# Reading the scalar 1.0 of VectorE's two-operand instructions from SBUF in a decoder layer

## The chip, the cores and the metric

The kernel runs on one core of one Trainium2 chip. The metric is the device time of one execution in microseconds (us), lower is better; the median of several runs counts. Five engines work side by side: TensorE (PE in the rows, with PEld for its weight loads), VectorE (DVE), ScalarE (ACT), GpSimd (POOL) and SyncE (SP), which issues all the DMAs of this kernel. Each takes its own instructions in order.

## What is computed

One decoder layer over 4096 positions of 1024 channels in float32. Two heads share one input projection: a causal depthwise convolution of width 31, and a spatial gate over chunks of 128 positions.

```
h = layer_norm(x)
a_val, a_gate, a_z, b_u, b_v, b_z = split(h @ w_in)          # six times 512 columns
y_a = silu(layer_norm(conv31(a_val * sigmoid(a_gate)))) * silu(a_z)
y_b = gelu(b_u) * (masked_ws @ layer_norm(gelu(b_v)) + b_s) * silu(b_z)
h = layer_norm(2**0.25 * h + concat(y_a, y_b) @ w_out)
out = h + sigmoid(h @ w_ple_gate + b) * (p @ w_ple)
```

## The kernel before

Five matrix products of 4096x1024 by 1024x1024 ("units" 0 to 4) run one after another, 16 pairs of 128-row tiles each. Every product is cut into quarters and done with seven block products in place of eight (Strassen's scheme in Winograd's form); `ORDER` names the seven. To hold float32 accuracy, each operand is split into a high and a low part, `ahi`/`alo` on the left and `whi`/`wlo` on the right, and three matmuls (lines 316 to 318) stand for one.

Three things are made on the side. The weights' seven combinations of the next unit are computed by GpSimd in `combos` (tile `bq`), stored in DRAM (`twD`) and fetched at the end of a unit by `load_operands` (tile `wst`), where ScalarE makes `whi` and VectorE `wlo` (`split_weight`). The left operands come by DMA (`qa`, `qb` from `qD`) or from transposed rows. The convolution (`conv`, lines 388 to 399) runs on VectorE with PSUM accumulators `acc`; its taps are per-partition scalars read from the SBUF tiles `cs_sb` and `cw_sb`. Tiles of the pool tag "big" (7 buffers, `wst`, `bq`, `qa`, `xr` and others) are shared by all stages.

A helper `ss` stands for `out = a op b` on two SBUF operands; it is written as VectorE's scalar_tensor_tensor, (a * 1.0) op b. It is called for `wlo` (two halves of 128x1024 for each weight operand), for the first combinations of weights (`wst`), for the rows of the first two pairs (`xr`), for the norm of v in unit 1 (`v`), for the low parts of the last product's small operands (`pl`, `wpl`, `wsx`), and for the last add of the output rows (`zr`). All of these appear in the trace as line 93, the helper's own.

The order of the instructions on each engine is not written out by hand. A scheduler of the language, with costs of its own for each instruction, orders the whole program when it is built, and chooses the buffers; a small change can reorder much of it.

Of the kernel before, what the change touches and what calls it, by code (L numbers as in the profile page):

```python
# [8 lines left out]
F32 = mybir.dt.float32  # L9
# [3 lines left out]
ADD, SUB, MUL = ALU.add, ALU.subtract, ALU.mult  # L13
# [3 lines left out]
P = 128  # L17
# [47 lines left out]
def hybrid_layer_kernel(  # L65
# [17 lines left out]
    nc = tc.nc  # L83
# [4 lines left out]
    stt = nc.vector.scalar_tensor_tensor  # L88
    ID = AF.Identity

    def ss(out, a, b, op):

        return stt(out, a, 1.0, b, op0=MUL, op1=op)  # L93

    const = ctx.enter_context(tc.tile_pool(name="const", bufs=1))
    dram = ctx.enter_context(tc.tile_pool(name="dram", bufs=1, space=DRAM))
# [28 lines left out]
    make_identity(nc, ident)  # L125
    nhalf = const.tile([P, 2], F32, name="nhalf")
    nc.gpsimd.memset(nhalf, -0.5)
    cw_sb = const.tile([P, CT, W31], F32, name="cw_sb")
    cs_sb = const.tile([P, CT, NE], F32, name="cs_sb")
    cb_sb = const.tile([P, CT], F32, name="cb_sb")  # L130
# [41 lines left out]
    def split_weight(stg):  # L172
        hi, lo = wtile("whi"), wtile("wlo")
        for c in range(2):
            cs = slice(2 * c, 2 * c + 2)
            act(hi[:, cs], stg[:, cs], ID)
            ss(flat(lo[:, cs]), flat(stg[:, cs]), flat(hi[:, cs].bitcast(F32)), op=SUB)
        return hi, lo
# [34 lines left out]
    def first_operands(W, stg):  # L213
        b11, b12, b22, b21 = (stg[ij] for ij in ((0, 0), (0, 1), (1, 1), (1, 0)))

        def sub(dst, a, b):
            for c in range(2):
                cs = slice(2 * c, 2 * c + 2)
                ss(flat(dst[:, cs]), flat(a[:, cs]), flat(b[:, cs]), op=SUB)

        W[1] = split_weight(b11)
        sub(b11, b12, b11)
        W[5] = split_weight(b11)
        W[3] = split_weight(b22)
        sub(b12, b22, b12)
        sub(b22, b22, b11)
        W[6] = split_weight(b22)
        W[7] = split_weight(b12)
        W[2] = split_weight(b21)
        sub(b21, b21, b22)  # L230
        W[4] = split_weight(b21)
# [239 lines left out]
    def first_rows():  # L471

        r = X[0]
        for j in (1, 0):
            mv = mvtile(1)
            moments([r[:, j, 0:C], r[:, j, C:]], mv[:, 0, :])
            nb = scale_bias(mv)
            act(r[:, j], r[:, j], ID, scale=mv[:, 0, 1:2], bias=nb[:, 0:1])
            for half in (0, 1):
                v = r[:, j, half * C : (half + 1) * C]  # L480
                ss(v, v, eb[:, 0, half * C : (half + 1) * C], op=MUL)
                ss(v, v, eb[:, 1, half * C : (half + 1) * C], op=ADD)
            dma(hT[0][j], r[:, j])
# [82 lines left out]
    for h in range(2):  # L566
        half = wsf[64 * h : 64 * (h + 1)].rearrange("p n (i m) -> p n i m", i=2)
        nc.gpsimd.affine_select(
            out=half, in_=half, pattern=[[0, NH], [1, 2], [2, 64]], compare_op=ALU.is_ge,
# [323 lines left out]
```

## Time and profile before

| | |
|---|---|
| median of 3 runs | 1895.17 us (1889.53 to 1897.29) |
| the profiled execution | 1896.8 us, of which its span is 1895.0 us |
| PE busy | 1802.0 us, 95% |
| DVE busy | 1405.1 us, 74%, 2176 instructions |
| POOL busy | 1270.2 us, 67% |
| ACT busy | 893.4 us, 47% |
| DMA | 362.07 MB, 55.4% of 16 engines' span |

The span is the time from the first to the last instruction in the profile; the execution's own time is 1.8 us longer. Busy times are averages over stages with different limits, so the chain of waits (what released the last instruction, followed back) says more of what a slower instruction costs.

### The profile page before, as it was taken

How to read it: one execution, taken by the hardware profiler on the slowest of the kernel's cores; microseconds unless marked ns; L12 is line 12 of the kernel's file. 1: busy time of each engine (PE TensorE's matmuls, PEld its weight loads, DVE VectorE, ACT ScalarE, POOL GpSimd, SP SyncE). 2: the span in 40 equal slices, each digit the busy share in tenths (PEclk: the TensorE clock that was granted, in tenths of full speed). 3: DMA queues.
4: the chain of work that ended last, by engine and by line, in shares of the span. 5: the costliest groups of instructions: out<-in, count | busy, mean ns of one | idle time of the engine just before them, and what ended most of it. 6: DMA issues, size and time to landing. Idle time of an engine off the chain costs nothing.

```text
span 1895.0 us, 24385 instructions
## 1 busy us (share of the span) xinstructions
PE 1802.0 (95%) x8322; PEld 1471.8 (78%) x8322; DVE 1405.1 (74%) x2176; ACT 893.4 (47%) x1438; POOL 1270.2 (67%) x1015
## 2 busy tenths in 40 slices
PE   5799999999999999999999798999999899999999
PEld 3687788877788887788888677787887688888887
DVE  8636887797787777989889976886568756655654
ACT  4655565565455555634445544455546322332222
POOL 2878987458786676588669567776677755655541
PEclk9899999999999999999999998999999999999999
DMA  6579776586734444899666856755446322222211
GB/s 240 193 233 352 254 231 214 182 297 210 239 112 148 138 160 150 304 353 328 211 200 222 308 192 228 250 186 191 168 167 236 119 101 78 89 90 95 100 55 52
DMA packets 184940, 363.62 MB, mean 192 GB/s; under 512 B 49648, under 2 KB 74224, under 8 KB 177136
## 3 DMA queue, kind: packets, MB, share of 16 engines
q1 hardware_dynamic: 184816, 362.07, 55.4%
q8 instruction: 66, 1.08, 0.2%
q14 instruction: 58, 0.48, 0.1%
HBM read 211.02 MB, written 150.99 MB: 191 GB/s over the span
## 4 chain that ended last, share of the span: by engine, by line
PE 75%; DVE 10%; DMA 7%; ACT 3%; issue 3%; POOL 2%; SPq 0%; DVEq 0%; POOLq 0%; ACTq 0%
PE pb L316 9%; PE pb L317 9%; PE pb L318 9%; PE pe L318 6%; PE pe L316 6%; PE pe L317 6%; PE pp L809 5%; PE tp L261 3%; PE pd L316 3%; PE pd L317 3%; PE pd L318 3%; PE pa L316 3%; PE pa L317 3%; PE pa L318 3%; DVE wlo L93 2%
## 5 line engine op out<-in xcount | busy, mean ns | idle before, releaser
L236 POOL TENSOR_TENSOR alo<-s,ahi 128x512 fp32r<-128x512 f32 x192 | 266.7, 1402 | 275.5 <-ACT ahi L235 271.6
L316 PE MATMUL pb<-whi,ahi 128*128 128x512 f32 x960 | 386.8, 403 | 13.2 <-ACT pa L334 5.4
L317 PE MATMUL pb<-wlo,ahi 128*128 128x512 f32 x960 | 379.3, 395 | 1.9 <-DVE wlo L93 1.9
L318 PE MATMUL pb<-whi,alo 128*128 128x512 f32 x960 | 379.0, 395 | 0.1
L316 PE MATMUL pe<-whi,ahi 128*128 128x512 f32 x640 | 257.0, 402 | 16.8 <-ACT ahi L235 7.5
L317 PE MATMUL pe<-wlo,ahi 128*128 128x512 f32 x640 | 253.3, 396 | 4.2 <-DVE wlo L93 4.0
L318 PE MATMUL pe<-whi,alo 128*128 128x512 f32 x640 | 255.5, 399 | 1.6 <-POOL alo L236 1.5
L316 PEld LDWEIGHTS pb<-whi,ahi 128*128 128x128 f32 x960 | 183.1, 191 | 57.0 <-ACT pa L334 9.0
L318 PEld LDWEIGHTS pb<-whi,alo 128*128 128x128 f32 x960 | 182.7, 190 | 40.0 <-POOL alo L236 0.5
L317 PEld LDWEIGHTS pb<-wlo,ahi 128*128 128x128 f32 x960 | 183.2, 191 | 38.8 <-DVE wlo L93 2.9
L236 POOL TENSOR_TENSOR alo<-qa,ahi 128x512 fp32r<-128x512 f32 x128 | 171.5, 1355 | 44.9 <-ACT ahi L235 44.8
L390 DVE SCALAR_TENSOR_TENSOR acc<-ca,cs_sb,acc 128x512 f32<-128x512 f32 x240 | 180.0, 750 | 4.1
L235 ACT ACTIVATE ahi<-s 128x512 fp32r<-128x512 f32 x192 | 119.9, 629 | 131.6 <-DVE s L288 49.7
L399 DVE SCALAR_TENSOR_TENSOR acc<-ca,cw_sb,acc 128x512 f32<-128x512 f32 x240 | 179.1, 746 | 0.8 <-POOL ca L383 0.6
L396 DVE SCALAR_TENSOR_TENSOR acc<-zy,cw_sb,acc 128x512 f32<-128x512 f32 x224 | 167.0, 746 | 2.6 <-POOL zy L382 1.5
L316 PEld LDWEIGHTS pe<-whi,ahi 128*128 128x128 f32 x640 | 121.8, 190 | 42.2 <-ACT ahi L235 8.7
L236 POOL TENSOR_TENSOR alo<-qb,ahi 128x512 fp32r<-128x512 f32 x96 | 126.9, 1328 | 39.6 <-ACT ahi L235 38.8
L317 PEld LDWEIGHTS pe<-wlo,ahi 128*128 128x128 f32 x640 | 121.7, 190 | 30.3 <-DVE wlo L93 6.5
L236 DVE TENSOR_TENSOR alo<-tp,ahi 128x512 fp32r<-128x512 f32 x144 | 97.9, 684 | 62.1 <-ACT ahi L235 60.0
L318 PEld LDWEIGHTS pe<-whi,alo 128*128 128x128 f32 x640 | 121.7, 190 | 26.8 <-POOL alo L236 2.5
L316 PE MATMUL pd<-whi,ahi 128*128 128x512 f32 x320 | 129.9, 406 | 5.5 <-ACT pd L334 3.8
L163 POOL TENSOR_TENSOR mv<-mv,nhalf 128x2 f32<-128x2 f32 (+1 forms) x81 | 55.4, 690 | 108.6 <-DVE mv L162 108.0
(147 smaller groups left out, 3994.7 us busy)
## 6 DMA issues: line engine op xcount, KB each, us to landing
qa<-qD SPq DMA_DIRECT2D x32, 1024.0 KB, 6.2
twD<-bq SPq DMA_DIRECT2D x112, 256.0 KB, 5.8
wst<-twD SPq DMA_DIRECT2D x28, 1024.0 KB, 7.2
qb<-qD SPq DMA_DIRECT2D x32, 768.0 KB, 6.5
xr<-in_x SPq DMA_DIRECT2D x32, 512.0 KB, 5.6
hT<-xr SPq DMA_DIRECT2D x32, 512.0 KB, 3.8
qD<-s SPq DMA_DIRECT2D x64, 256.0 KB, 2.9
bq<-in_wq SPq DMA_DIRECT2D x64, 256.0 KB, 5.0
```

The lines of the kernel that those rows point to most:

```text
L93: return stt(out, a, 1.0, b, op0=MUL, op1=op)
L163: ptt(mv[:, :, 1], mv[:, :, 1], nhalf[:, 0:n], op=ALU.pow)
L235: act(hi, src, ID)
L236: eng.tensor_tensor(lo, src, hi.bitcast(F32), op=SUB)
L261: nc.tensor.transpose(out=tp[:, kk * P : (kk + 1) * P], in_=rows[:, j, k * P : (k + 1) * P], identity=ident,)
L316: nc.tensor.matmul(ps, lhsT=ah[:, k, :], rhs=wh[:, k, :], start=start and k == 0, stop=False, **kw)
L317: nc.tensor.matmul(ps, lhsT=ah[:, k, :], rhs=wl[:, k, :], start=False, stop=False, **kw)
L318: nc.tensor.matmul(ps, lhsT=al[:, k, :], rhs=wh[:, k, :], start=False, stop=k == 3, **kw)
L390: stt(even, src, w, even, op0=MUL, op1=ADD)
L396: stt(dst, src, cw_sb[:, ct, 2 * k + 1 : 2 * k + 2], odd if k else even, op0=MUL, op1=ADD)
L399: stt(src if k == NE - 1 else even, src, cw_sb[:, ct, 2 * k : 2 * k + 1], even, op0=MUL, op1=ADD,)
L809: nc.tensor.matmul(pp, lhsT=l[:, k, ts], rhs=r[:, k, cs], start=k == 0 and l is ph and r is wp_hi, stop=k == 1 and l is pl,)
```

## The change

The helper's immediate 1.0 becomes a pointer to a 128x1 tile `one`, which GpSimd fills once at the start.

```diff
     def ss(out, a, b, op):
 
-        return stt(out, a, 1.0, b, op0=MUL, op1=op)
+        return stt(out, a, one, b, op0=MUL, op1=op)
...
     nhalf = const.tile([P, 2], F32, name="nhalf")
     nc.gpsimd.memset(nhalf, -0.5)
+    one = const.tile([P, 1], F32, name="one")
+    nc.gpsimd.memset(one, 1.0)
     cw_sb = const.tile([P, CT, W31], F32, name="cw_sb")
```

Lines behind the new tile have numbers two higher in the changed kernel.

In the built program the tile `one` takes 32 bytes of each partition, so nearly every SBUF tile lies 32 bytes higher: the first tile of the tag "big" begins at byte 2016 of the partition before and at byte 2048 now, and the others of that tag follow at steps of 8192. The built program also has another order in places: 406 lines of difference in VectorE's 2178 rows, 1290 in TensorE's 8324, 142 in SyncE's 841. Two places follow.

On VectorE, at the end of the start phase, before: the last rows of the second pair's layer norm (`xr`, four instructions of 128x1024) and the last low parts of unit 0's weights (`wlo`).

```order
L162 TENSOR_SCALAR mv<-mv 128x2
L152 BN_AGGR mv<-st 128x2 x2
L93 SCALAR_TENSOR_TENSOR wst<-wst 128x1024 x2
L162 TENSOR_SCALAR mv<-mv 128x2
L93 SCALAR_TENSOR_TENSOR xr<-xr,eb 128x1024 x3
L93 SCALAR_TENSOR_TENSOR wlo<-wst,whi 128x1024
L93 SCALAR_TENSOR_TENSOR xr<-xr,eb 128x1024
L93 SCALAR_TENSOR_TENSOR wlo<-wst,whi 128x1024
```

The same place of the changed kernel, with `one` among the operands:

```order
L164 TENSOR_SCALAR mv<-mv 128x2
L154 BN_AGGR mv<-st 128x2
L93 SCALAR_TENSOR_TENSOR wst<-wst,one 128x1024
L154 BN_AGGR mv<-st 128x2
L93 SCALAR_TENSOR_TENSOR wst<-wst,one 128x1024
L164 TENSOR_SCALAR mv<-mv 128x2
L93 SCALAR_TENSOR_TENSOR xr<-xr,one,eb 128x1024
L93 SCALAR_TENSOR_TENSOR wlo<-wst,one,whi 128x1024
L93 SCALAR_TENSOR_TENSOR xr<-xr,one,eb 128x1024 x2
L93 SCALAR_TENSOR_TENSOR wlo<-wst,one,whi 128x1024
L93 SCALAR_TENSOR_TENSOR xr<-xr,one,eb 128x1024
```

The last of the four `xr` instructions stood behind one `wlo` and now stands behind two.

On SyncE, early in unit 1, before: `uD` stores the gate's tile `g`, `qa` and `qb` fetch the left operands of a coming pair, `bq` and `twD` belong to the weights' combinations.

```order
L187 DMA bq<-in_wq 128x512 x4
L590 DMA uD_133<-g_4170 128x4x512
L190 DMA twD_174<-bq 128x512
L242 DMA qa<-qD_113 128x2048
L190 DMA twD_174<-bq 128x512 x2
L243 DMA qb<-qD_113 128x1536
L192 DMA twD_174<-bq 128x512
L195 DMA twD_174<-bq 128x512
```

The same place now:

```order
L189 DMA bq<-in_wq 128x512 x4
L192 DMA twD_176<-bq 128x512
L244 DMA qa<-qD_115 128x2048
L592 DMA uD_135<-g_4172 128x4x512
L192 DMA twD_176<-bq 128x512 x2
L194 DMA twD_176<-bq 128x512
L197 DMA twD_176<-bq 128x512
L245 DMA qb<-qD_115 128x1536
```

The store `uD` has moved behind the fetch of `qa`, and the fetch of `qb` behind two more stores of `twD`.

## Rows read from the trace of the kernel before

**Rows 1.** The page: busy times, and the chain that ended last by engine.

```profile
PE 1802.0 (95%) x8322; PEld 1471.8 (78%) x8322; DVE 1405.1 (74%) x2176; ACT 893.4 (47%) x1438; POOL 1270.2 (67%) x1015
PE 75%; DVE 10%; DMA 7%; ACT 3%; issue 3%; POOL 2%; SPq 0%; DVEq 0%; POOLq 0%; ACTq 0%
```

**Rows 2.** Windows: start phase and last unit, all engines (columns in the first line).

```profile
core 0: us, PE busy (x) PEld busy (x) DVE busy (x) ACT busy (x) POOL busy (x), PEclk, DMA share, GB/s
0.00:60.00 60.00, 27.00 (x83) 18.75 (x84) 51.58 (x65) 28.89 (x34) 22.07 (x26) 0.89 0.55 200
...
1480.00:1895.00 415.00, 404.51 (x1865) 330.98 (x1863) 248.15 (x336) 115.74 (x194) 215.33 (x114) 0.99 0.24 83
```

**Rows 3.** One line, L93: durations min/median/max in ns, by tile.

```profile
L93 DVE SCALAR_TENSOR_TENSOR wlo<-wst,whi x70: 1164/1218/3379, 13.7 to 1475.4; 128x1024 fp32r<-128x1024 f32 x70
L93 DVE SCALAR_TENSOR_TENSOR v<-v,sgb x64: 655/693/1784, 438.9 to 769.2; 128x512 f32<-128x512 f32 x64
L93 DVE SCALAR_TENSOR_TENSOR zr<-zr,c x32: 682/1372/2893, 1488.7 to 1885.9; 128x512 f32<-128x512 f32 x32
```

**Rows 4.** Windows of L93 alone, whole span: busy us (instructions), PEclk, DMA share, GB/s.

```profile
0.00:1895.00 1895.00, 273.37 (x237) 0.98 0.56 192
```

**Rows 5.** The whole chain of waits: its first and last L93 piece (start us, us).

```profile
10.10 0.04 DVE xr L93
...
1891.42 0.69 DVE zr L93
```

**Rows 6.** Groups by line and form on DVE: busy us, mean ns, idle before.

```profile
L390 DVE SCALAR_TENSOR_TENSOR acc<-ca,cs_sb,acc 128x512 f32<-128x512 f32 x240 | 180.0, 750 | 4.1
L388 DVE TENSOR_SCALAR acc<-ca,cs_sb,cb_sb 128x512 f32<-128x512 f32 x16 | 12.9, 805 | 4.1 <-DMA ca<-aD 4.1
L399 DVE SCALAR_TENSOR_TENSOR ca<-ca,cw_sb,acc 128x512 f32<-128x512 f32 x16 | 11.8, 735 | 0.0
L338 DVE SCALAR_TENSOR_TENSOR pa<-hr,pb 128x512 f32<-128x512 f32 x16 | 11.1, 694 | 13.1 <-PE pb L318 13.1
L338 DVE SCALAR_TENSOR_TENSOR s<-hr,pe 128x512 f32<-128x512 f32 x16 | 10.8, 678 | 1.6 <-POOL alo L236 1.0 <-issue 0.6
```

**Rows 7.** One line, L390, a pointer scalar with one SBUF stream: min/median/max ns.

```profile
L390 DVE SCALAR_TENSOR_TENSOR acc<-ca,cs_sb,acc x240: 695/755/758, 167.2 to 1229.6; 128x512 f32<-128x512 f32 x120
```

**Rows 8.** Timeline of DVE at the change of unit 0 to 1.

```profile
400.67 0.74 DVE L396 SCALAR_TENSOR_TENSOR acc<-zy,cw_sb,acc 128x512 f32<-128x512 f32 x1
401.32 0.74 DVE L399 SCALAR_TENSOR_TENSOR acc<-ca,cw_sb,acc 128x512 f32<-128x512 f32 x1
```

**Rows 9.** Chain of waits at the end of the start phase.

```profile
54.47 1.14 DVE wlo L93
55.60 3.30 DVE xr L93
59.33 5.62 DMA xr<-in_x
```

**Rows 10.** Waits of SP's queue, longest first: us in total, times, longest.

```profile
SPq L497 <- DVE xr L93: 24.1, 2, 20.1
```

**Rows 11.** Chain of waits early in unit 1.

```profile
486.84 5.99 DMA uD<-g
492.85 6.89 DMA qb<-qD
...
511.14 8.35 DMA qa<-qD
```

**Rows 12.** Windows early in the last unit, columns as in rows 2.

```profile
1497.00:1501.00 4.00, 0.99 (x7) 0.60 (x5) 3.91 (x3) 0.32 (x1) 4.00 (x3) 0.91 0.35 129
1501.00:1506.00 5.00, 4.76 (x11) 3.81 (x12) 2.31 (x3) 0.27 (x1) 1.80 (x1) 0.50 0.15 56
```

**Rows 13.** Timeline of PE after that idle time.

```profile
1501.24 0.80 PE L316 MATMUL pe<-whi,ahi 128*128 128x512 f32 x1 [3.25 <-DVE s L336]
```

## The prediction

> **What bounds the kernel now.** I read the page's busy times and its chain first, then the stages, then line 93, which is all that the change touches. TensorE is busy for 95% of the span and holds 75% of the chain that ended last; VectorE holds 10% of it and DMA 7% [rows 1]. So a slower VectorE instruction costs time only where VectorE is in that chain. The stages say where that can be: in the first 60 us VectorE is busy for 51.58 us and TensorE for 27.00, so there VectorE sets the pace; in the last unit TensorE is busy for 404.51 of 415 us and VectorE for 248.15, so there 167 us of VectorE's time are free [rows 2].
>
> Line 93 has 237 instructions, 273.37 us in all [rows 4]. Most are 128x1024 (median 1218 ns for the 70 of `wlo`) or 128x512 (median 693 ns for the 64 of `v`), but many take far longer: the 32 of `zr` with `c` have a median of 1372 ns for the same size, and single ones reach 3379 [rows 3]. 85 instructions at 1.22 us and 152 at 0.69 would make 208 us, so some 65 us are waiting inside the instruction. In the whole chain I count 75 of the 237, the first at 10.10 us and the last at 1891.42 [rows 5]: 27 in the first 60 us, 43 at and around the changes of unit and in the norm of v, 5 behind 1480 us.
>
> **The change, part by part.** One memset of a 128x1 tile on GpSimd, some nanoseconds before anything waits for it, since the first line-93 instruction starts at 10.10 us [rows 5]: nothing. No operation and no byte of DMA is added elsewhere.
>
> *The pointer.* The trace has no instruction with two SBUF streams and a pointer scalar, so its price is bounded by neighbours with one SBUF and one PSUM stream of the same 128x512. With a pointer and a result in PSUM: 750 ns (L390); with an immediate: 694 (L338, `pa`). With a pointer and a result in SBUF: 735 (L399, `ca`); with an immediate: 678 (L338, `s`). Both pairs differ by 56 to 57 ns, and the tensor_scalar with two pointers takes 805, that is 55 above the one with one [rows 6]. The price shows in the pitch too: two convolution taps start 0.65 us apart (400.67 and 401.32) though the first lasts 0.74 [rows 8]; a `wlo`, 1.22 us long in the median, gives way after 1.13 (54.47 to 55.60) [rows 3, 9], so about 0.08 us at an instruction's end is shared with the next one whether it has a pointer or not, and the price isn't hidden in that. Below, the price may be nothing, if with two SBUF streams the pointer is read while the streams are set up; above, I see no single row beyond 57 ns save the waits inside the instruction, which are a rival. I take 57 ns, since the same operation and engine show it twice.
>
> [...]
>
> On VectorE's busy time the price is 237 x 57 ns = 13.5 us. On the chain it is 75 x 57 ns = 4.3 us. The other 162 are covered: in the last unit by TensorE, which runs on through the output adds (404.51 of 415 us) [rows 2]; in the norm of v and in the weights by work of TensorE's that stands ready. If that cover were gone everywhere, the bound is 13.5 us.
>
> *The order.* At the end of the start phase the last `xr` instruction stands behind two `wlo` in place of one. That place is in the chain: `wlo`, the last `xr`, then the fetch of the next rows at 59.33 us [rows 9], because SP's queue stands at the store of these rows (line 497, 24.1 us in two waits) and the fetch is queued behind it [rows 10]. One more `wlo` ahead costs its pitch, 1.14 us [rows 9]. It isn't a loss for sure: the same `wlo` is no longer to be done behind the `xr`; the bounds are nothing and 1.14, and I take 1.1, since the fetch is what the chain follows. Early in unit 1, SyncE now issues `uD` behind `qa`, and `qb` behind two more stores. The chain goes through these DMAs (5.99, 6.89 and 8.35 us [rows 11]), and an issue moved past two others shifts by a microsecond at most either way; I put it at nothing, with 1 us of doubt. The many other swaps have no sign that I can read, and are a rival.
>
> The sum against the profiled execution: 1896.8 + 4.3 + 1.1 = 1902.2 us. That execution lies 1.6 us above the median of the three runs, so against the median the forecast is **1900.6 us**, 0.3% above 1895.17. I take about 0.5% (9.5 us: below 1885.7 or above 1904.7) as what this kernel's measurement can tell from no change, so the forecast is "same".
>
> **Rivals.**
>
> *The pointer waits for GpSimd as well (slower).* The waiting inside line 93 (65 us on 237 instructions, 274 ns each) falls on instructions with two SBUF streams. If the read of the pointer has to get past GpSimd's work like a stream, each instruction could wait once more: 75 x 274 ns = 20.6 us on the chain, 1896.8 + 20.6 = 1917.4, or 1916 against the median. It decides from 127 ns per instruction (9.5 us over 75). Against it: the 240 taps of L390 read a pointer from SBUF while GpSimd is busy for 67% of the span, and none took over 758 ns [rows 1, 7]. [...] Chance 0.10.
>
> *The tiles' new place makes DMAs shorter (faster).* All tiles of the tag "big" now begin at a multiple of 2048 bytes and no longer 32 bytes below one. DMA has 7% of the chain [rows 1], some 133 us. No tile of the kernel before begins at a multiple of 64, so no row gives a price. The gain reaches the 0.5% if it undoes 5.4 us and takes off 9.5 more, 14.9 us of 133: 11% of every DMA in the chain. At that it gives 1885.7; at half of it 1893. Of the three in rows 11, 21.2 us, it would take off 2.4. [...] Chance 0.12 that it is felt, 0.08 that it passes the 0.5%.
>
> *The new order opens holes on TensorE (slower).* [...] Chance of one more, 0.13; of one fewer, 0.07.
>
> *The pointer is free with two streams.* The sum is 1.1 us, 1896 against the median. This stays inside "same". Chance 0.08.
>
> **How the numbers follow.** The forecast, with its own range of 1895 to 1905, has the remaining 0.50. Holding eight in ten takes in the free pointer, half of the DMA gain and one hole opened or closed: from 1890 up to 1909. Left out are the waits behind GpSimd and a DMA gain over the whole chain, together with two holes. Chances: faster by over 0.5% 0.08 (the DMA gain), slower 0.21 (GpSimd 0.10, most of the hole's 0.13), same 0.71.
>
> **What the next profile would show.** Line 93's undisturbed instructions at about 750 ns (512) and 1275 (1024), VectorE's busy time at about 1419 us, and `zr` with `c` still long. If medians stay at 693 and 1218, the pointer is free; if the mean waits grow by more than 100 ns, GpSimd's rival holds. The landing times of `wst`, `qa` and `twD` tell of the tiles' place; the windows with a granted clock of 0.50 tell of holes. The forecast is wrong above all if the new order matters more than the pointer, since I can price only two of its many swaps.

## The result and the profile after

The changed kernel takes 1911.56 us (median of 6 runs, 1902.61 to 1913.71), the kernel before, run beside it on the same chip, 1894.8 us (1889.53 to 1898.48). The ratio is 1.0082, with a 95% interval of 1.0065 to 1.0099. So it is slower by 16.8 us, above the forecast of 1900.6 and above the end of its range at 1909.0. Single executions of some kernels below were disturbed and took 2576 to 3643 us; they are left out of every median and ratio, and the trace of place_only, which is one of them, is not read.

The page of the changed kernel, with the lines that answer to [rows 1]:

```profile
span 1909.6 us, 24394 instructions
...
PE 1806.9 (95%) x8322; PEld 1475.4 (77%) x8322; DVE 1417.7 (74%) x2176; ACT 894.1 (47%) x1438; POOL 1272.2 (67%) x1016
...
PE 77%; DVE 9%; DMA 5%; POOL 4%; issue 3%; ACT 2%; SPq 0%; DVEq 0%; POOLq 0%; ACTq 0%
```

VectorE's busy time rose by 12.6 us, close to the 13.5 that 57 ns on 237 instructions would make. The span rose by 14.6 us, and VectorE's share of the chain fell from 10% to 9%. The extra time on VectorE is there, then, but the chain doesn't show it as the cause.

Line 93 by tile, durations min/median/max in ns, beside [rows 3]:

```profile
L93 DVE SCALAR_TENSOR_TENSOR wlo<-wst,one,whi x70: 1226/1276/3515, 14.3 to 1489.7; 128x1024 fp32r<-128x1024 f32 x70
L93 DVE SCALAR_TENSOR_TENSOR v<-v,one,sgb x64: 729/752/1840, 441.1 to 770.6; 128x512 f32<-128x512 f32 x64
L93 DVE SCALAR_TENSOR_TENSOR zr<-zr,one,c x32: 750/1317/2194, 1506.5 to 1900.5; 128x512 f32<-128x512 f32 x32
```

The medians of `wlo` and `v` rose by 58 and 59 ns. `zr` with `c`, which takes about twice as long as `v` at the same 128x512, did not rise: 1372 ns before, 1317 now.

The first large difference in time is at the end of the start phase. The timeline there (start, duration in us) of VectorE, then of GpSimd, whose first `xr` rows of the third pair begin here, and of TensorE's next work (the last number is its idle time, and what ended it), after:

```profile
54.34 1.28 DVE L93 SCALAR_TENSOR_TENSOR wlo<-wst,one,whi 128x1024 fp32r<-128x1024 f32 x1
55.53 2.48 DVE L93 SCALAR_TENSOR_TENSOR xr<-xr,one,eb 128x1024 f32<-128x1024 f32 x2
57.93 3.37 DVE L93 SCALAR_TENSOR_TENSOR wlo<-wst,one,whi 128x1024 fp32r<-128x1024 f32 x1
61.21 3.36 DVE L93 SCALAR_TENSOR_TENSOR xr<-xr,one,eb 128x1024 f32<-128x1024 f32 x1
...
57.34 6.15 POOL L497 TENSOR_TENSOR xr<-xr,eb 128x1024 f32<-128x1024 f32 x2 [4.01 <-ACT xr L496]
...
64.72 2.94 PE L263 MATMUL tp<-ident,xr 128*128 128x128 f32 x12 [10.94 <-DVE xr L93]
```

And before:

```profile
54.39 1.21 DVE L93 SCALAR_TENSOR_TENSOR wlo<-wst,whi 128x1024 fp32r<-128x1024 f32 x1
55.53 3.36 DVE L93 SCALAR_TENSOR_TENSOR xr<-xr,eb 128x1024 f32<-128x1024 f32 x1
58.81 3.38 DVE L93 SCALAR_TENSOR_TENSOR wlo<-wst,whi 128x1024 fp32r<-128x1024 f32 x1
...
55.14 5.97 POOL L495 TENSOR_TENSOR xr<-xr,eb 128x1024 f32<-128x1024 f32 x2 [4.01 <-ACT xr L494]
...
59.04 2.94 PE L261 MATMUL tp<-ident,xr 128*128 128x128 f32 x12 [9.43 <-DVE xr L93]
```

TensorE transposes these rows (`tp`) once the last `xr` is done. Before, that was at 59.04 us; after, at 64.72 us. The last `xr` stands behind one more `wlo`, as forecast. That `wlo`, which begins after GpSimd's rows have begun, lasts 3.37 us, where the one at 54.34, ahead of them, takes 1.28. Before, it stood behind the last `xr`, and lasted 3.38 us there too.

### The profile page after: what moved, and what is told of

Same layout as the page of the kernel before. It is cut to its first block, busy times and chain, and to the rows that moved or that the text cites. A ratio compares the mean times of both kernels' runs of the same rounds, so it can differ in the third digit from the quotient of the medians.

```text
span 1909.6 us, 24394 instructions
## 1 busy us (share of the span) xinstructions
PE 1806.9 (95%) x8322; PEld 1475.4 (77%) x8322; DVE 1417.7 (74%) x2176; ACT 894.1 (47%) x1438; POOL 1272.2 (67%) x1016
## 4 chain that ended last, share of the span: by engine, by line
PE 77%; DVE 9%; DMA 5%; POOL 4%; issue 3%; ACT 2%; SPq 0%; DVEq 0%; POOLq 0%; ACTq 0%
PE pb L318 10%; PE pb L319 9%; PE pb L320 9%; PE pe L320 6%; PE pe L318 6%; PE pe L319 6%; PE pp L811 5%; PE tp L263 3%; PE pd L318 3%; PE pd L319 3%; PE pd L320 3%; DVE wlo L93 3%; PE pa L318 3%; PE pa L319 3%; PE pa L320 3%
## 5 line engine op out<-in xcount | busy, mean ns | idle before, releaser
L238 POOL TENSOR_TENSOR alo<-s,ahi 128x512 fp32r<-128x512 f32 x192 | 262.8, 1380 | 265.4 <-ACT ahi L237 261.7
```

The lines of the kernel that those rows point to most:

```text
L238: eng.tensor_tensor(lo, src, hi.bitcast(F32), op=SUB)
```

## The experiments

What changed at once is a pointer operand, a new order of the program, and a new place of the SBUF tiles. The scheduler's order follows from the form of the operand alone: a program with the tile and its memset, but immediates, is built in the order of before. My theory after the result was that the order costs most of it and the pointer about 4 us; the rivals were the pointer (16 us, through waits) and the place.

To tell them apart, an order was held while the operand was exchanged: the program is built and ordered with one operand, and then the scalar of each instruction in question is replaced in the finished list, with its semaphores as they were.

**imm_new_order: the order and place of the change, with immediates.**

```diff
+def with_scalar(i, scalar):
+    I = type(i)
+    return I(
...
+        ins=[i.ins[0], scalar, i.ins[2]], outs=list(i.outs), sync_info=i.sync_info,
...
+    for block in nc.main_func.blocks:
+        block.instructions = [
+            with_scalar(i, _mybir.ImmediateValue(dtype=F32, value=1.0))
+            if getattr(i, "is_scalar_tensor_tensor", False)
+            and str(getattr(i.ins[1], "memref", "")).startswith("one") else i
+            for i in block.instructions
+        ]
```

> The changed program with its order, buffers and tile places, but every line-93 instruction given back the immediate 1.0 after the ordering. Order theory (the new order costs about 10 us, the pointer 4 to 5, the tiles' place nothing): 1905 us, ratio 1.005. Pointer theory (the pointer's 57 ns per instruction cost the whole 16 us, because more of the 237 come onto the path than the 75 counted): 1895 to 1897, ratio 1.000. Place theory (tiles 32 bytes higher cost the 10 us): 1905 here too, and in the run with the place alone.

Measured: 1906.91 us, ratio 1.0064 (1.0042 to 1.0087), 11.7 us above the kernel before beside it (1895.23). So without a single pointer at run time, some 12 of the 16.8 us stay.

**ptr_old_order: the order of before, with pointers.** The program is built with `1.0`, and the same replacement puts `one` in.

> The order of before, with the pointer put into all 237 line-93 instructions after the ordering; the tile one exists, so tiles lie 32 bytes higher. Order theory: only the pointer's price on the chain, 1899 to 1900, ratio 1.0025. Pointer theory: 1908 to 1911, ratio 1.008. Place theory: 1909.

Measured: 1897.37 us, ratio 1.0011 (0.9998 to 1.0025), somewhat less than the order theory's 1899 to 1900. Line 93 carries the pointer's price, as in the changed kernel:

```profile
L93 DVE SCALAR_TENSOR_TENSOR wlo<-wst,one,whi x70: 1225/1277/3374, 13.7 to 1471.3; 128x1024 fp32r<-128x1024 f32 x70
L93 DVE SCALAR_TENSOR_TENSOR v<-v,one,sgb x64: 718/752/1789, 435.7 to 768.2; 128x512 f32<-128x512 f32 x64
```

So the price of each instruction is real, and little of it reaches the end.

**place_only: the tile `one` and its memset, but immediates.** The scheduler then makes the order of before, so only the tiles' place differs.

```diff
     nc.gpsimd.memset(nhalf, -0.5)
+    one = const.tile([P, 1], F32, name="one")
+    nc.gpsimd.memset(one, 1.0)
```

> The tile one and its memset exist, nothing reads them: immediates and order of before, tiles 32 bytes higher. Order theory and pointer theory: 1895, ratio 1.000. Place theory: 1905, ratio 1.005; or, if the new place helps DMAs, below 1890.

Measured: 1893.49 us, ratio 0.9986 (0.9971 to 1.0002): no difference that this tells from nothing. ptr_old_order differs from it by the pointer alone: 1897.4 - 1893.5 = 3.9 us.

**ptr_old_place: the pointer and the new order, tiles at their old place.** The ones stand in a third column of `nhalf`, which takes no more room.

```diff
-        return stt(out, a, 1.0, b, op0=MUL, op1=op)
+        return stt(out, a, nhalf[:, 2:3], b, op0=MUL, op1=op)
...
-    nhalf = const.tile([P, 2], F32, name="nhalf")
+    nhalf = const.tile([P, 3], F32, name="nhalf")
```

> The ones stand in a third column of the tile nhalf, so no tile moves; pointers and order are those of the changed kernel. Order theory and pointer theory: 1911, ratio 1.008, as the changed kernel. Place theory: 1900, ratio 1.003.

Measured: 1911.47 us, ratio 1.0090 (1.0071 to 1.0109), the changed kernel's time. The place is out.

**Parts of the order.** In three kernels only some calls carry the pointer while the scheduler works, and all are immediates at run time. imm_start_order has the start phase and unit 0 ordered as after; the second half of unit 1, the change to unit 2, unit 2 and the last unit from 1600 us on are as before, and the rest has an order of its own. imm_rest_order has the start phase as before, and by its trace the order of after in the second half of unit 2 and from 1250 us, in unit 3, on. imm_unit1_order (pointer in the two calls of the norm of v) differs from before in unit 1, in the change to unit 2 and in the first half of unit 2. The edit of imm_rest_order:

```diff
     def ss(out, a, b, op):
-        return stt(out, a, one, b, op0=MUL, op1=op)
+        return stt(out, a, scalar[0], b, op0=MUL, op1=op)
+
+    scalar = [1.0]
...
+    scalar[0] = one
```

> Immediates everywhere at run time; the order is the one that the scheduler makes when only the start phase's line-93 instructions carry the pointer: start phase ordered as in the changed kernel, unit 0 too, later stretches ordered anew or as before. Theory that each loss has its place: 5 us late at the first pair of unit 0, of which about half is left at the end of unit 0, so 1896 to 1898, ratio 1.001 to 1.002, whatever comes later kept aside. Rival (any new order costs the same dozen us, wherever it differs): 1905 to 1908, ratio 1.006.

> Immediates everywhere at run time; the order made when all but the start phase's instructions carry the pointer: start phase as before, from the middle of unit 2 on the same order as the changed kernel's. Theory that each loss has its place: nothing lost at the first pair, a loss of some 4 us at the change to unit 2 and of 4 to 5 us early in unit 4, so 1902 to 1904, ratio 1.004 to 1.005. Rival (the start's 5 us are what is carried to the end): 1895 to 1897, ratio 1.000.

> Immediates everywhere at run time; the order made when only the norm of v in unit 1 carries the pointer: only unit 1 and the change to unit 2 are ordered anew. Theory that each loss has its place: up to 4 us at the change to unit 2, 1895 to 1899, ratio 1.000 to 1.002. Rival (any new order costs a dozen): 1905 to 1908.

Measured: imm_start_order 1895.98 us, 1.0016 (1.0006 to 1.0026); imm_rest_order 1899.08, 1.0025 (1.0011 to 1.0040); imm_unit1_order 1897.52, 1.0022 (1.0002 to 1.0042). No part carries the whole loss. imm_rest_order missed both of its expectations: it lies between the theory's 1902 to 1904 and the rival's 1895 to 1897. Start with unit 0, and the stretches that imm_rest_order takes from after, share no part of the new order; together they make 0.41% of 0.64%, so if parts add up, 0.23% (4.4 us) is left for unit 1, the change to unit 2 and the first part of unit 3. That is an estimate: each of these kernels also has stretches in an order that neither before nor after has.

**short_rows_new and short_rows_old: is the start's loss contention with GpSimd?** In both orders, with immediates, GpSimd's four `xr` instructions behind these rows are cut to 8 elements, which leaves out part of the first layer norm.

```diff
+    rows = [
+        i.name for block in nc.main_func.blocks for i in block.instructions
+        if str(i.engine).endswith("Pool") and type(i).__name__ == "InstTensorTensor"
+        and str(i.outs[0].memref).startswith("xr")
+    ][:4]
+    for block in nc.main_func.blocks:
+        block.instructions = [shorter(i) if i.name in rows else i for i in block.instructions]
```

> Order of the changed kernel with immediates; GpSimd's four instructions on the rows of the third pair (xr, 128x1024) do only 8 elements of each row, so part of the first layer norm is left out. If the moved wlo and the last xr are long because GpSimd's rows run beside them, each falls from 3.36 to about 1.2 us and TensorE's first transposes behind them come some 4.3 us earlier, at about 60.2 us in place of 64.6. If they are long for another reason, they stay at 3.36.

> Order of before, the same four instructions cut to 8 elements. The last xr falls from 3.36 to about 1.2 us and TensorE's first transposes come at about 56.9 us in place of 59.0; so the two orders then differ by about 3.3 us at that point (2.2 from the later norm and 1.1 from the plain pitch of one wlo) in place of 5.5.

One execution each: 1899.06 and 1893.5 us. VectorE and TensorE in short_rows_new_t, the same kernel as short_rows_new in a later run (below), at the place of the two timelines above:

```profile
53.47 2.35 DVE L93 SCALAR_TENSOR_TENSOR xr<-xr,eb 128x1024 f32<-128x1024 f32 x2
55.74 1.22 DVE L93 SCALAR_TENSOR_TENSOR wlo<-wst,whi 128x1024 fp32r<-128x1024 f32 x1
56.88 1.22 DVE L93 SCALAR_TENSOR_TENSOR xr<-xr,eb 128x1024 f32<-128x1024 f32 x1
...
58.24 2.94 PE L263 MATMUL tp<-ident,xr 128*128 128x128 f32 x12 [8.41 <-DVE xr L93]
```

And in short_rows_old_t, the order of before with the same cut:

```profile
55.23 1.22 DVE L93 SCALAR_TENSOR_TENSOR xr<-xr,eb 128x1024 f32<-128x1024 f32 x1
56.37 1.22 DVE L93 SCALAR_TENSOR_TENSOR wlo<-wst,whi 128x1024 fp32r<-128x1024 f32 x1
...
56.60 2.94 PE L261 MATMUL tp<-ident,xr 128*128 128x128 f32 x12 [7.24 <-DVE xr L93]
```

With GpSimd's rows cut the `wlo` and the `xr` take 1.22 us each, not 3.36, and the transposes of the two orders start 1.6 us apart (58.24 and 56.60; 0.8 us in the single executions, 57.82 and 57.05). So contention with GpSimd makes the two instructions long: shown. Uncut, imm_new_order starts the transposes at 64.57, 5.5 us behind the 59.04 of before, but not all of that is the order. 3.3 us are the moved `wlo` (57.79 to 61.07). The other 2.2 go with a fetch of the second pair's rows that was issued at 31.44 us in this execution and at 29.00 before. imm_start_order has the same start phase and immediates, with the fetch at 28.88, and its transposes start 3.3 us behind those of before:

```profile
55.57 3.37 DVE L93 SCALAR_TENSOR_TENSOR wlo<-wst,whi 128x1024 fp32r<-128x1024 f32 x1
58.86 3.35 DVE L93 SCALAR_TENSOR_TENSOR xr<-xr,eb 128x1024 f32<-128x1024 f32 x1
...
62.36 1.94 PE L265 MATMUL tp<-ident,xr 128*128 128x128 f32 x8 [12.65 <-DVE xr L93]
```

So the order is worth 3.3 us here, against 0.8 and 1.6 with the rows cut; the expected 3.3 with the cut counted the 2.2 us of the fetch as the order's. Whether this is the loss at the end, single executions could not say, so both cut kernels were timed.

> The order of the change with immediates, and GpSimd's four xr instructions of the third pair cut to 8 elements (that part of the first layer norm is left out): the kernel of the earlier single look, now timed. If the loss of the order is the contention at the end of the start phase, the two orders with the cut come to within 3 us of each other, about 1894. If half of the start's 5 us is made up later anyway, as the progress of the earlier profiles suggests, the cut takes off about 5 of the 12.4 us and this kernel stands 7 us (0.4%) above its counterpart, about 1901. If the start has nothing to do with the time at the end, 12 us stay and it comes out near 1907.

> The order of before with the same cut (part of the first layer norm left out), timed: 0 to 3 us below the kernel before, since its own last xr is disturbed as well (3.36 us in place of 1.2), so about 1892 by every theory. The difference to the kernel with the order of the change is what counts.

Measured: 1900.17 us, 1.0035 (1.0019 to 1.0052), and 1891.0 us, 0.9984 (0.9972 to 0.9996). With the cut the orders are 9.2 us apart, without it 11.7. I had named three outcomes, 3, 7 and 12 us; this one lies between the second and the third. The start's contention can be some 2.5 us of the loss, and, given the intervals, also nothing. imm_start_order, with the whole of the start's new order and the rows uncut, agrees: 0.16% (3 us) in all. It isn't the main part.

**imm_wlo_order: yet another order.** Here only `split_weight` in `load_operands` carries the pointer while the order is made; immediates at run time. 289 lines of VectorE's order and 981 of TensorE's differ from before, and the end of the start phase does not.

> Immediates at run time; the order is the one the scheduler makes when only the wlo of the weight operands carry the pointer. Its start phase has the wlo and xr at the end as the kernel before, and behind them 289 lines of VectorE's order and 981 of TensorE's differ. If the loss is tied to the start's swap and the change from unit 1 to 2 in particular, this one stays within 0.25% of before (up to 1899). If any other order than that of before costs several tenths of a per cent, it lies at 0.3 to 0.7%, 1900 to 1908. If orders scatter to both sides, it may be below 1894.

Measured: 1894.9 us, 1.0013 (0.9998 to 1.0029). So a large reordering need not be costly.

## Where the order's time went

Windows of the same times show TensorE's work (behind the window stand its length and TensorE's busy time; the third number from the end is the granted clock). First the kernel before, then after, then imm_new_order, then ptr_old_order:

```profile
0.00:66.00 66.00, 32.83 (x104) 23.02 (x104) 56.00 (x69) 34.23 (x43) 28.07 (x28) 0.87 0.59 211
...
770.00:820.00 50.00, 48.87 (x224) 39.88 (x223) 46.02 (x68) 27.06 (x43) 35.52 (x29) 1.00 0.91 321
```

```profile
0.00:66.00 66.00, 28.72 (x84) 19.35 (x85) 55.92 (x65) 29.06 (x35) 23.73 (x28) 0.86 0.51 184
...
770.00:820.00 50.00, 45.24 (x201) 36.78 (x200) 43.68 (x61) 27.76 (x42) 34.81 (x23) 0.97 0.86 322
```

```profile
0.00:66.00 66.00, 28.06 (x85) 19.77 (x86) 52.87 (x65) 29.04 (x35) 26.06 (x28) 0.88 0.51 185
...
770.00:820.00 50.00, 45.26 (x203) 37.42 (x202) 42.27 (x62) 25.46 (x39) 34.94 (x27) 0.97 0.89 333
```

```profile
0.00:66.00 66.00, 30.89 (x97) 21.38 (x97) 57.70 (x67) 33.17 (x41) 25.98 (x29) 0.87 0.58 204
...
770.00:820.00 50.00, 49.65 (x228) 41.07 (x228) 46.85 (x71) 25.98 (x42) 38.69 (x30) 1.00 0.93 322
```

Beside the kernel before, the two with the new order lose 4 to 5 us of TensorE's time in the start phase and 3.6 us at the change from unit 1 to unit 2; the pointer in the old order loses 2 us at the start and nothing at the change. The second window doesn't hold the same work in all four: by the last pair of unit 1 the new order is already 3 to 7 us behind. In imm_new_order the waits at that change are (TensorE, last number the idle time before and what ended it):

```profile
756.59 0.50 PE L318 MATMUL pb<-whi,ahi 128*128 128x512 f32 x1 [2.29 <-ACT whi L178]
758.50 0.50 PE L319 MATMUL pb<-wlo,ahi 128*128 128x512 f32 x1 [1.41 <-DVE wlo L93]
...
773.53 0.58 PE L585 MATMUL sp<-vl,wsx 128*128 128x256 f32 x1 [2.56 <-POOL vl L611]
...
788.17 0.50 PE L318 MATMUL pe<-whi,ahi 128*128 128x512 f32 x1 [2.17 <-ACT ahi L237]
```

Before, the longest waits between 740 and 800 us are 1.1 to 1.35 us each; two of them:

```profile
748.19 0.50 PE L316 MATMUL pd<-whi,ahi 128*128 128x512 f32 x1 [1.35 <-ACT pd L334]
...
766.43 0.50 PE L317 MATMUL pe<-wlo,ahi 128*128 128x512 f32 x1 [1.17 <-DVE wlo L93]
```

The order moved which operands of the first unit-2 matmuls are late: `whi` from ScalarE, the low part `vl` of the norm of v from GpSimd, and `ahi` of the first pair.

Waiting is only part of what this change costs. Windows of 5 us around the first two waits, in imm_new_order and then before:

```profile
745.00:750.00 5.00, 5.00 (x24) 4.07 (x22) 4.46 (x7) 3.19 (x6) 5.00 (x5) 1.00 0.55 197
750.00:755.00 5.00, 3.33 (x14) 2.17 (x12) 4.58 (x11) 2.63 (x5) 3.82 (x5) 1.00 1.00 305
755.00:760.00 5.00, 2.00 (x6) 1.38 (x7) 4.02 (x5) 4.35 (x6) 4.90 (x5) 0.95 1.04 372
760.00:765.00 5.00, 5.00 (x17) 3.99 (x16) 5.00 (x8) 3.79 (x5) 0.37 (x1) 0.71 0.85 287
```

```profile
755.00:760.00 5.00, 3.60 (x12) 2.10 (x12) 5.00 (x8) 3.81 (x6) 1.44 (x2) 1.00 0.87 278
760.00:765.00 5.00, 3.32 (x12) 2.10 (x12) 4.18 (x7) 2.62 (x5) 2.68 (x3) 1.00 0.85 326
765.00:770.00 5.00, 3.83 (x16) 2.78 (x16) 5.00 (x6) 3.75 (x5) 0.30 (x1) 1.00 0.70 269
```

In the new order TensorE works for only 2.00 of the 5 us from 755 to 760, and then the granted clock drops to a mean of 0.71 (over 3800 windows of 0.5 us of the changed kernel's trace, from 0 to 1900 us, it reads 1.00 in 3645, 0.50 in 131 and a value between in 24): TensorE is busy all the time from 760 to 765 and gets through 17 instructions, where it gets through 24 at 1.00, from 745 to 750 us. Before, the shorter waits are spread out and the clock stays at 1.00.

To compare the same work over the whole span I set marks: the start of the add of line 354 (356 with the tile) in each of the 80 pairs, for five profiles with the whole new order (after, imm_new_order, ptr_old_place and the two with cut rows) and four with the order of before (before, ptr_old_order and the two with cut rows). Here is how much more the first group took than the second, mean against mean, each relative to the kernel before:

| stretch | new order minus old, us | the five | the four |
|---|---|---|---|
| to the first pair of unit 0, rows not cut | +4.5 | 5.0 to 5.2 | 0.0 and 1.2 |
| the same, rows cut | +1.2 | -1.7 and -1.3 | -2.9 and -2.4 |
| unit 0 | -0.3 | -3.0 to -0.5 | -3.2 to 0.0 |
| unit 1 | +1.6 | 0.7 to 3.2 | -0.1 to 1.1 |
| last pair of unit 1 to third pair of unit 2 | +2.9 | 0.6 to 4.6 | -1.0 to 0.0 |
| rest of unit 2 | +0.1 | -0.6 to 0.4 | -1.1 to 0.4 |
| unit 3 | +1.5 | -2.9 to 2.1 | -2.9 to 0.0 |
| last pair of unit 3 to fifth pair of unit 4 | +3.6 | 2.1 to 4.6 | -1.8 to 1.6 |
| unit 3 and this change together | +5.1 | 1.7 to 4.2 | -3.0 to 0.0 |
| rest of unit 4 | -1.5 | -0.2 to 1.3 | 0.0 to 4.5 |

Three places stand clear of the scatter between executions: the end of the start phase, the change 1 to 2, and unit 3 with the change 3 to 4. Unit 3 and its change belong together, since the order moved work over the mark: TensorE begins 572 instructions in that change in each of the four and 584 or 594 in the five; in unit 3 it begins 1629 in the four and 1609 or 1619 in the five. The three places sum to 12.5 us (9.2 with the rows cut), the rest to about nothing. That is near the measured 11.7 and 9.2 us, though these are single executions, and the first row holds more than the order: imm_start_order, with the start's new order, is 2.9 us late there. (Two of the five and one of the four carry the pointer, so it weighs about alike in both groups.)

What the start's part is made of is shown. At the change 1 to 2, TensorE's busy time grew by 1.9 us (two instructions more, some 0.5 us, are part of that) and its idle time by 1.0. In this stretch the mean granted clock is 0.93 to 0.95 in each of the five, and 1.00 in each of the four. So more of this part goes with the lower clock, which follows the waits, than with the waiting itself. The timed runs agree: over all of them the granted clock has a mean of 0.982 to 0.983 in the four kernels with the whole new order, and of 0.985 to 0.988 in all others. But that is read from traces: no experiment took a wait away; in ptr_old_place the wait for `vl` is missing and the time is the same, so that wait alone isn't it. And imm_rest_order, in yet another order there, is 3.0 us longer in this stretch at a clock of 1.00, by waiting alone. For unit 3 and the change 3 to 4 no single wait is found.

## Why the prediction was wrong, by its own steps

**The pointer** was right in price, and its sum fits. Forecast: 57 ns for an instruction, 4.3 us at the end. Measured: 58 and 59 ns in the medians, and 3.9 us at the end with the order held (1897.4 against 1893.5); with the new order held, 1.0090 against 1.0064, 4.9 us, or 3.4 us by the changed kernel's own 1.0082. The bound of 13.5 us without cover isn't reached, so most of the other 162 instructions were covered; the count of 75 itself was not tested.

**The step that failed is "The order".** It was put at 1.1 us and measured some 12 (11.7 with immediates). It has two parts. The first, "One more `wlo` ahead costs its pitch, 1.14 us", took its price from another `wlo`, the one at 54.47, which ran ahead of GpSimd's `xr` rows. The one that moved ahead of the last `xr` is the next, at 58.81, and beside these rows it lasted 3.38 us already. At its new place it is still beside them, and lasts 3.37 us. So the transposes came 3.3 us later by the order (imm_start_order), not 1.1. The rows for this were at hand: the `xr` from 55.60 took 3.30 us [rows 9] where its neighbours take 1.2, and the `wlo` next to it had to be priced the same way. With GpSimd's rows cut to 128x8 (short_rows_new_t), the two instructions took 1.22 us each in place of 3.36. The prediction weighed a wait behind GpSimd for the pointer alone.

The second part was the larger one: "The many other swaps have no sign that I can read, and are a rival", at a chance of 0.13 for one hole. The range up to 1909 counts one hole in, and no run shows what a hole costs at the end; the trace of before shows a wait of 3.25 us [rows 13] and 5 us at a granted clock of 0.50 behind it [rows 12], and the runs showed several smaller losses in its place. No part-order costs as much as the whole, and the loss lies in several places. At the change 1 to 2 the first operands of the next unit are late, TensorE waits 2.3 and 1.4 us close together, and the granted clock then falls (0.71 from 760 to 765 us); in all it costs 2.9 us by the marks. So the rival "The new order opens holes on TensorE" came true at this change, at too small a chance, and with two shorter waits where the kernel before has one of 3.25 us. Unit 3 and the change 3 to 4 make another 5.1 us, whose cause isn't found. The profile gave a sign of where a swap can cost: the 43 of 75 chain instructions that the prediction itself counted around the changes of unit and in the norm of v.

**SyncE's swaps** in unit 1 (`uD`, `qa`, `qb`), put at nothing, with a microsecond of doubt: `qb` is issued 4.98 us behind `qa` before (487.87 and 492.85 us in the trace) and 9.02 us behind it now (489.24 and 498.26), a shift of 4 us. Unit 1 as a whole is 1.6 us longer by the marks, not clear of the scatter; no run tests these swaps by themselves, so this stays open.

**The rivals.** "The pointer waits for GpSimd as well" (1916 us) gave nearly the measured time and is still not the cause: `zr` with `c` got no longer in the changed kernel (1317 ns), and ptr_old_order carries every pointer at 1.0011. "The tiles' new place": no run shows the DMA gain, half of which the range down to 1890 counts in; no gain or loss can be told, 0.9986 (0.9971 to 1.0002) and, with the old place, the changed kernel's own time. "The pointer is free": no, 58 ns an instruction and about 4 us.

**What stays open.** Which swaps make the change 1 to 2 and unit 3 with its change longer isn't settled: the new order moves `whi`, `wlo`, `vl` and the left operands at once, and a single swap can't be undone without the scheduler moving others.

## What to carry to other kernels

Where a scheduler orders the program, an operand that changes its cost table changes the order, and that can outweigh the operand: here 12 us against 4. Separate the two, by exchanging the operand after the order is made, before blaming either. And price an instruction that moves by its own row and by what runs beside it, not by another of its kind: here a VectorE instruction with two SBUF operands took 3.36 us beside GpSimd's rows of 128x1024 and 1.22 with these rows cut to 128x8. At a change of stage, look for late first operands, and read the granted clock behind them: at the change 1 to 2 TensorE's busy time grew by 1.9 us at a mean clock of 0.93 to 0.95, more than its idle time (1.0).

## What the runs showed of the hardware

A pointer scalar adds 58 to 59 ns to a scalar_tensor_tensor on two SBUF streams at 512 and at 1024 elements alike (medians of `v` 693 and 752 ns, of `wlo` 1218 and 1276), so at these two lengths it is a price of the instruction and not of its length; before, only neighbours with a PSUM stream showed it. And the same instructions in five other orders, with immediates at run time, gave ratios of 1.0013, 1.0016, 1.0022, 1.0025 and 1.0064: the order alone is worth up to 0.64% among these.
